# Weight sums in two half buffers, one-input softmax statistics, loads on ACT's queue and C21 of a pair in PSUM, in a one-core diffusion step

## The chip, the cores and the metric

The kernel runs on one core of a Trainium2 chip. The metric is the device time of one execution in microseconds (us). The engines are called PE (TensorE), PEld (its weight loads), DVE (VectorE), ACT (ScalarE), POOL (GpSimd) and SP (SyncE, which here only issues transfers).

## The reference, cut to what matters

One layer with two head groups that read the same normalised input: a gated position-mixing MLP (group A) and latent attention with four heads (group B). Their outputs are concatenated, go through the output projection `w_o`, are gated and added to the residual, and the rows are normalised.

```python
def _back(x, gate, a_out, attn, g_b, w_o):
    y = jnp.concatenate([a_out, attn * jax.nn.silu(g_b)], axis=-1) @ w_o
    return x + gate * y
...
    attn = _block_attention(qn, (qr_rot, qr), ((kn, kr_rot, vv), (kn_c, kr_c, v_c)))
    xs = _back(xs, gate, a_out, attn, g_b, w_o[l])
y_prompt = _rmsnorm(xp, final_g)
y_sample = _rmsnorm(xs, final_g)
```

There are 1024 latent rows (8 tiles of 128), 128 context rows (tile 8) and 256 cached keys. All is float32.

## The kernel before, in words

Products are made in three passes over a high and a low part of each operand (`hi` is a rounded copy, `lo = x - hi`), so nearly every product has a copy (ACT or POOL) and a subtraction (DVE) ahead of it.

**Softmax and value stage** (lines 1450 to 1780, some 317 to 540 us of the span). For each of 32 heads (8 tiles x 4), PE makes logits against 1024 latent and 256 context keys. `softmax` takes two maxima on DVE (L1480, L1483), joins them to the bias `nb` (L1484), ACT makes two exponentials with their sums (L1490), DVE adds the sums and inverts them (L1494, L1495), and POOL scales the row `e` (L1496). `value_steps` transposes `e` on PE (L1557), splits the result into `ph` (ACT, L1561) and `pl` (DVE, `lo_of`, L112), multiplies by the values (L1581 to L1583) and projects (L1600). The order on each engine is the order in which the program issues instructions. It is written by hand: every step has a cost, `later(dt, fn)` puts a step off by that much planned time, and `merged` mixes two lists of steps in proportion to their costs. An engine then runs its instructions in that order, each as soon as what it needs is there.

**Weight sums**. The output projection of the latent tiles is done on pairs of tiles by a scheme with seven products instead of eight (A11, A12, S4, S2, S1, S3, A22) on sums of blocks of `w_o`. The four sums T1 to T4 are made during the softmax stage, in 16 pieces, the *units* `(u, part)`: u counts eight slices of `w_o`, a part is two subtractions on POOL (`t_unit`, `sub`, L809). The raw slices lie in the tile `traw` (two buffers). After part 1 the kernel copies the high parts into `thi` (ACT, L1883), subtracts in place (DVE, L112) and stores both parts to `tdram` with eight transfers on SP (L1880). `divide`, once per head, starts the units: one and two in turn, as long as there are any. The tile pool of the sums is closed after head 17, and then the pieces of plain `w_o` are loaded and split, as *jobs* in the list `his` (copies on POOL) and `los` (subtractions on DVE), a few per head. Jobs of `w_o` have rank 0 and go ahead of others.

**Start of the last stage**. The context tile 8 is projected in the plain way, `plain(k, i)` for k of eight weight blocks and i of two column halves, into two PSUM banks `wps[8]`; the first two products of pair 0 are made beside it (the list `early`, mixed with the last two value streams). `t_piece` and `t_fetch` load the weight sums back from `tdram`, issued by POOL (L1901, L1905): T2 early, T3 after `plain(4, 1)`, T1 and T4 at the start of the last stage. Gates, the rows `xr` and `final_g` are loaded by SP (L1987, L2047, L2059).

**Last stage** (from line 2015, 536 us to the end). A small planner, `Plan`, holds steps with an engine, a planned cost, what they depend on, a priority and resources they take and give. At each planned instant it issues the first step in order of priority whose engine is free, whose inputs are made and whose resources are left. It only fixes the order of issue. Resource `w` counts PSUM banks (pool `psw`, five banks), `raw` PSUM copies of blocks, engine `D` the loads, which follow each other every 1.35 planned us (`fetch`). For each pair `pair(n)` makes seven products on PE; the queue of split blocks runs up to five ahead (`hi`, `raw`, `lo` of queue entry q). DVE adds the products up to C11, C12, C22 and C21 (`c11`, `c12`, `c22`, `c21`), each is gated (`m..`) and added to its row (`a..`), mostly on POOL, and ACT squares the row for the norm (`square`, L2078). `norm` makes the root, and `y` scales the two rows (DVE, L2110) and stores them. The last pair has another order and an end written out by hand (`finish`, L2260 to L2305).

```python
on_v(D_("c21"), lambda: add(V, K, ps("A22"), K), [P_("A22"), D_("k7")], 2, gives=("w",))
on_g(D_("m21"), lambda: G.tensor_tensor(K, K, gL(), op=ALU.mult), [D_("c21"), "gate0"], 3)
on_g(D_("a21"), lambda: add(G, half(b, L), half(b, L), K), [D_("m21"), f"x{b}"], 3)
square(b, 1, lambda: K, L, [D_("a21")])
```

Of the kernel before, what the change touches and what calls it, by code (L numbers as in the profile page):

```python
# [18 lines left out]
P = 128  # L19
# [75 lines left out]
def tile_hymba_step(ctx: ExitStack, tc: tile.TileContext, I, O):  # L95
# [1374 lines left out]
    def softmax(t, h, lat_, con_):  # L1470

        m = sm.tile([P, 2], F32, tag="m", name=f"m{t}{h}", bufs=3)
        nb = sm.tile([P, 1], F32, tag="nb", name=f"nb{t}{h}", bufs=3)
        su = sm.tile([P, 2], F32, tag="su", name=f"su{t}{h}", bufs=3)
        rs = sm.tile([P, 1], F32, tag="rs", name=f"rs{t}{h}", bufs=3)
        e = ap_.tile([P, 1280], F32, tag="e", name=f"e{t}{h}", bufs=6)
        es[t, h] = e

        def start():
            V.tensor_reduce(m[:, 0:1], lat_, axis=AX.X, op=ALU.max)  # L1480

        def shift():
            V.tensor_reduce(m[:, 1:2], con_, axis=AX.X, op=ALU.max)  # L1483
            V.scalar_tensor_tensor(nb, m[:, 0:1], m[:, 1:2], nscl[:, t : t + 1], op0=ALU.max, op1=ALU.mult)  # L1484
            later(0.6, exps)
            later(1.3, lambda: spare_lo(1))

        def exps():
            for i, (src, sl) in enumerate(((con_, slice(1024, 1280)), (lat_, slice(0, 1024)))):
                S.activation(e[:, sl], src, AF.Exp, bias=nb, scale=scl[:, t : t + 1], accum_out=su[:, i : i + 1])  # L1490
            later(2.5 if t == 0 or (t, h) < (1, 2) else 1.9, divide)

        def divide():
            V.tensor_tensor(rs, su[:, 0:1], su[:, 1:2], op=ALU.add)  # L1494
            V.reciprocal(rs, rs)  # L1495
            G.tensor_scalar(e, e, rs, 0.0, op0=ALU.mult, op1=ALU.add)  # L1496
            made.add(("e", t, h))
            spare_hi(2)
            spare_lo(2)
            if units and units[0][0] in traw:  # L1500
                n_ = min(len(units), (1, 2)[paced[0] % 2])
                paced[0] += 1
                for _ in range(n_):
                    unit_of[0](*units.pop(0))

        return start, shift
# [276 lines left out]
    with tc.manual_schedule(engines=engines):  # L1783
# [73 lines left out]
        th, tl = {}, {}  # L1857
# [7 lines left out]
        def t_unit(u, part):  # L1865

            k, c = divmod(u, 2)
            raw = traw[u]
            b11, b12, b21, b22 = (raw[:, i, :] for i in range(4))
            if part == 0:  # L1870
                sub(G, b11, b12, b11)
                sub(G, b12, b22, b12)
                return
            sub(G, b22, b22, b11)
            sub(G, b21, b21, b22)
            hi = tp.tile([P, 4, 256], F32R, tag="hi", name=f"thi{u}")

            def store(i, src):
                for m, j in ((1, 0), (3, 1), (4, 2), (2, 3)):
                    nc.sync.dma_start(f32(tdram[m - 1, k][:, i, 256 * c : 256 * c + 256]), src[:, j, :])  # L1880

            def high(i):
                S.copy(hi[:, 2 * i : 2 * i + 2, :], raw[:, 2 * i : 2 * i + 2, :])  # L1883
                if i:
                    store(0, f32(hi))

            def low(i):
                lo_of(raw[:, 2 * i : 2 * i + 2, :].bitcast(F32R), raw[:, 2 * i : 2 * i + 2, :], hi[:, 2 * i : 2 * i + 2, :])
                if i:
                    store(1, raw)  # L1890
                    if u + 2 < 8:
                        t_load(u + 2)
# [52 lines left out]
        for c in range(len(pairs)):  # L1945
# [18 lines left out]
            if 2 * c + LEAD + 1 == 17:  # L1964
# [20 lines left out]
        def load_xr(t):  # L1985
            xr[t] = ep.tile([P, 1024], F32, tag="xr", name=f"xr{t}", bufs=4)
            nc.sync.dma_start(xr[t], I["x"][t])  # L1987
# [37 lines left out]
    plan.resources.update(w=1, raw=2)  # L2025
# [9 lines left out]
    def on_g(key, fn, deps, prio, cost=1.3, **kw):  # L2035
        step(key, "G", cost, fn, deps, prio, lag=0.15, **kw)
# [8 lines left out]
    def load_gate(cond, **kw):  # L2045
        gate[cond] = ep.tile([P, 1024], F32, name=f"gate{cond}", **kw)
        nc.sync.dma_start(  # L2047
# [11 lines left out]
    fetch("fg", lambda: nc.sync.dma_start(fg, I["final_g"].broadcast_to([P, 1024])))  # L2059
# [29 lines left out]
    def norm(g, prio, by_half=False):  # L2089
# [17 lines left out]
        for i, u in enumerate(g):  # L2107
# [5 lines left out]
            if not by_half:  # L2113
                on_v(f"y{u}", scale, [*prev, "fg"], prio, 1.25)
# [49 lines left out]
    def pair(n):  # L2164
# [46 lines left out]
        if last:  # L2211
# [3 lines left out]
            step(f"free{n}", "N", 0.0, lambda: None, [f"sq{a}.0"], 0, gives=("w",))  # L2215
# [6 lines left out]
        if not last:  # L2222
# [9 lines left out]
            on_v(D_("c21"), lambda: add(V, K, ps("A22"), K), [P_("A22"), D_("k7")], 2, gives=("w",))  # L2232
            on_g(D_("m21"), lambda: G.tensor_tensor(K, K, gL(), op=ALU.mult), [D_("c21"), "gate0"], 3)
            on_g(D_("a21"), lambda: add(G, half(b, L), half(b, L), K), [D_("m21"), f"x{b}"], 3)
            square(b, 1, lambda: K, L, [D_("a21")])
# [176 lines left out]
```

## Time and profile before

| | us |
|---|---|
| three runs | 626.41, 629.21, 631.53 (median 629.21) |
| the profiled execution: time, span | 629.55, 627.8 |
| PE busy | 600.1 of the span |
| DVE, ACT, POOL busy | 427.5, 329.9, 218.1 |
| granted TensorE clock, mean | 0.992 |

In the rows of a timeline stand the start (us from the span's start), the duration, the engine, the line, the operation, output and inputs, shapes, and in brackets the idle time of the engine before it with what ended it. Rows of one line that follow each other are merged and counted (x2). In the rows of windows stand the window, its length, the busy time of PE, PEld, DVE, ACT and POOL with the number of instructions, the granted clock, the share of the 16 transfer engines and GB/s. Matmuls are pipelined: a PE that is busy all the time issues a 512-column matmul every 0.23 us, though each lasts 0.39.

### The profile page before, as it was taken

The page shows a single profiled execution, that of the slowest core. Times are in us where ns is not written, and L with a number is a line of the kernel's source. Part 1 is how long each engine was busy: PE and PEld are TensorE (multiplying, and loading weights), DVE is VectorE, ACT ScalarE, POOL GpSimd, SP SyncE. Part 2 cuts the span into 40 slices and gives each one's busy share as a digit, 9 for nine tenths or more (in the row PEclk, how much of TensorE's full clock was granted, in tenths as well). Part 3 has the DMA queues.
Part 4 walks back from the last instruction along what each step waited for, and adds up shares of the span by engine and source line. Part 5 has one row for each costly group of instructions (what it writes and reads, how often), then busy time and mean ns, then how long its engine had stood idle before and what let it go on. Part 6 is the DMA issues. An engine that isn't in the chain of part 4 may idle for free. (4 is left out here: it accounts for less than half of the span.)

```text
span 627.8 us, 10196 instructions
## 1 busy us (share of the span) xinstructions
PE 600.1 (96%) x3659; PEld 538.9 (86%) x3659; DVE 427.5 (68%) x911; ACT 329.9 (53%) x765; POOL 218.1 (35%) x261
## 2 busy tenths in 40 slices
PE   8899999999999999999999989899999999989992
PEld 7578889999989999999988978789999988768882
DVE  4784458896855567566778677786766855458765
ACT  6556754336423354555675656566555443456543
POOL 2451111000000000433462455552332566558772
PEclk9999999999999999999999999999999999989997
DMA  8992000101261034000020063651101028944222
GB/s 318 389 367 72 1 33 2 34 1 67 101 232 62 11 119 131 13 1 1 6 69 1 27 215 130 202 167 35 68 2 34 33 85 267 367 154 168 88 101 114
DMA packets 31922, 67.33 MB, mean 107 GB/s; under 512 B 3440, under 2 KB 18560, under 8 KB 31360
## 3 DMA queue, kind: packets, MB, share of 16 engines
q1 hardware_dynamic: 28560, 57.50, 26.5%
q0 software_dynamic: 2880, 8.39, 4.1%
q10 hardware_dynamic: 432, 0.79, 0.3%
q8 instruction: 29, 0.48, 0.3%
q14 instruction: 21, 0.17, 0.1%
HBM read 53.45 MB, written 13.21 MB: 106 GB/s over the span
## 5 line engine op out<-in xcount | busy, mean ns | idle before, releaser
L1496 POOL TENSOR_SCALAR e<-e,rs 128x1280 f32<-128x1280 f32 x32 | 46.2, 1444 | 105.5 <-DVE rs L1495 49.3
L112 DVE TENSOR_TENSOR pl<-pT,ph 128x512 fp32r<-128x512 f32 x81 | 55.4, 687 | 39.3 <-ACT ph L1561 37.9
L1490 ACT ACTIVATE e<-s,nb,scl 128x256 f32<-128x256 f32 x64 | 56.1, 880 | 39.8 <-DVE nb L1484 39.8
L1561 ACT CAST ph<-pT 128x512 fp32r<-128x512 f32 x80 | 46.0, 587 | 35.4 <-PE pT L1557 31.7
L1237 POOL TENSOR_TENSOR kr<-z,rope 128x64 f32<-128x64 f32 x8 | 2.6, 322 | 172.5 <-ACT z L1246 172.5
L1557 PE MATMUL pT<-ident,e 128*128 128x128 f32 x320 | 48.4, 274 | 6.8 <-DVE pl L112 6.8
L752 PE MATMUL tp<-area,w 128*128 128x384 f32 x288 | 52.4, 338 | 0.0
L752 PEld LDWEIGHTS tp<-area,w 128*128 128x128 f32 x288 | 50.3, 188 | 0.4
L1581 PE MATMUL o<-ph,vh 128*128 128x256 f32 x160 | 47.7, 298 | 0.0
L1557 PEld LDWEIGHTS pT<-ident,e 128*128 128x128 f32 x320 | 37.1, 140 | 12.1 <-PE at L1600 4.0
L1583 PE MATMUL o<-ph,vl 128*128 128x256 f32 x160 | 45.2, 282 | 0.0
L1582 PE MATMUL o<-pl,vh 128*128 128x256 f32 x160 | 45.1, 282 | 0.0
L1480 DVE TENSOR_REDUCE m<-s 128x1 f32<-128x1024 f32 x32 | 38.9, 1216 | 1.5 <-PE s L1514 1.5
L1510 PE MATMUL s<-kch,area 128*128 128x512 f32 (+2 forms) x100 | 39.0, 390 | 0.0
L1513 PE MATMUL s<-krh,area 128*128 128x512 f32 (+2 forms) x100 | 35.4, 354 | 0.0
L1511 PE MATMUL s<-kcl,area 128*128 128x512 f32 (+2 forms) x100 | 35.3, 353 | 0.0
L1512 PE MATMUL s<-kch,area 128*128 128x512 f32 (+2 forms) x100 | 35.2, 352 | 0.0
L1514 PE MATMUL s<-krl,area 128*128 128x512 f32 (+2 forms) x100 | 35.2, 352 | 0.0
L976 PE MATMUL tp<-area,w 128*128 128x384 f32 x192 | 35.0, 337 | 0.0
L976 PEld LDWEIGHTS tp<-area,w 128*128 128x128 f32 x192 | 33.6, 188 | 0.4 <-issue 0.4
L1581 PEld LDWEIGHTS o<-ph,vh 128*128 128x128 f32 x160 | 30.4, 190 | 1.6
L1582 PEld LDWEIGHTS o<-pl,vh 128*128 128x128 f32 x160 | 30.4, 190 | 1.4
(660 smaller groups left out, 1731.3 us busy)
## 6 DMA issues: line engine op xcount, KB each, us to landing
ada<-in_ada_ss SPq DMA_DIRECT2D x16, 512.0 KB, 8.5
w2r<-in_w_t SPq DMA_DIRECT2D x12, 512.0 KB, 4.5
x<-in_x SPq DMA_DIRECT2D x9, 512.0 KB, 7.9
xr<-in_x SPq DMA_DIRECT2D x9, 512.0 KB, 8.5
adag<-in_ada_g SPq DMA_DIRECT2D x4, 1024.0 KB, 5.0
traw<-in_w_o SPq DMA_DIRECT2D x16, 256.0 KB, 3.4
tdram<-thi SPq DMA_DIRECT2D x32, 128.0 KB, 3.0
tdram<-traw SPq DMA_DIRECT2D x32, 128.0 KB, 2.1
```

The lines of the kernel that those rows point to most:

```text
L112: V.tensor_tensor(lo, src, f32(hi), op=ALU.subtract)
L752: T.matmul(tps[i, g][:, :GW], w_[i][:, k, :], x_[k, g], start=k == 0 and j == 0, stop=k == NK - 1 and j == 2)
L976: T.matmul(tps[c, 2][:, :GW], w_[c][:, k, :], x_[k, 2], start=k == 0 and m == 0, stop=k == NK - 1 and m == 2)
L1480: V.tensor_reduce(m[:, 0:1], lat_, axis=AX.X, op=ALU.max)
L1490: S.activation(e[:, sl], src, AF.Exp, bias=nb, scale=scl[:, t : t + 1], accum_out=su[:, i : i + 1])
L1496: G.tensor_scalar(e, e, rs, 0.0, op0=ALU.mult, op1=ALU.add)
L1510: T.matmul(ps, qh_, kch[:, sl], start=True, stop=False)
L1557: T.transpose(ps[:, w : w + P], es[t, h][:, c * P : (c + 1) * P], ident)
L1561: later(0.5, lambda: S.copy(ph[:, :w], ps[:, :w]))
L1581: T.matmul(o, vh[:, kt, :], ph[:, sl], start=c == 0, stop=False)
L1582: T.matmul(o, vh[:, kt, :], pl[:, sl], start=False, stop=False)
L1583: T.matmul(o, vl[:, kt, :], ph[:, sl], start=False, stop=c == n - 1)
```

## The change

1. While there are units, the join of two maxima and the sum of two exponential sums, which read two tensors, become reductions over the two columns; the factor of `nb` is an instruction of its own.
2. The high copies of a unit get a tile for each half (`hi0`, `hi1`), and stores go out by half. The first half is copied 3.6 planned us after part 0, the rest after part 1. Units are started 1, 1, 1, 2 per head instead of 1, 2; the second of two is put off by 2.2. The pool is closed after head 19.
3. `plain(0..3, 1)` come first in `early`, and T3 is fetched by four jobs of `his`, entered after `plain(3, 1)` behind the jobs of rank 0.
4. Gates, rows 8, 0 and 1 and `final_g` are issued by ACT instead of SP.
5. C21 of pairs 0 to 2 is added up in the PSUM bank of A22, gated and added to its row by DVE, and the bank is given back after the square.
6. A resource `lock` of one keeps planned POOL steps and the scaling of output rows `y` apart.

```diff
         def shift():
             V.tensor_reduce(m[:, 1:2], con_, axis=AX.X, op=ALU.max)
-            V.scalar_tensor_tensor(nb, m[:, 0:1], m[:, 1:2], nscl[:, t : t + 1], op0=ALU.max, op1=ALU.mult)
+            if units:
+                V.tensor_reduce(nb, m, axis=AX.X, op=ALU.max)
+                V.tensor_scalar(nb, nb, nscl[:, t : t + 1], None, op0=ALU.mult)
+            else:
+                V.scalar_tensor_tensor(nb, m[:, 0:1], m[:, 1:2], nscl[:, t : t + 1], op0=ALU.max, op1=ALU.mult)
...
         def divide():
-            V.tensor_tensor(rs, su[:, 0:1], su[:, 1:2], op=ALU.add)
+            if units:
+                V.tensor_reduce(rs, su, axis=AX.X, op=ALU.add)
+            else:
+                V.tensor_tensor(rs, su[:, 0:1], su[:, 1:2], op=ALU.add)
...
-                n_ = min(len(units), (1, 2)[paced[0] % 2])
+                n_ = min(len(units), (1, 1, 1, 2)[paced[0] % 4])
                 paced[0] += 1
-                for _ in range(n_):
-                    unit_of[0](*units.pop(0))
+                for i in range(n_):
+                    unit_of[0](*units.pop(0), 2.2 * i)
...
-        def t_unit(u, part):
+        def t_unit(u, part, more):
...
+            def store(i, part_, src):
+                for m, j in ((1, 0), (3, 1), (4, 2), (2, 3))[2 * i : 2 * i + 2]:
+                    nc.sync.dma_start(f32(tdram[m - 1, k][:, part_, 256 * c : 256 * c + 256]), src[:, j % 2, :])
+
+            def high(i):
+                his_[u, i] = tp.tile([P, 2, 256], F32R, tag=f"hi{i}", name=f"thi{u}{i}")
+                S.copy(his_[u, i], raw[:, 2 * i : 2 * i + 2, :])
+                store(i, 0, f32(his_[u, i]))
+
+            def low(i):
+                half = raw[:, 2 * i : 2 * i + 2, :]
+                lo_of(half.bitcast(F32R), half, his_[u, i])
+                store(i, 1, half)
+                if i and u + 2 < 8:
+                    t_load(u + 2)
+
             if part == 0:
                 sub(G, b11, b12, b11)
                 sub(G, b12, b22, b12)
+                later(3.6 + more, lambda: high(0))
                 return
             sub(G, b22, b22, b11)
             sub(G, b21, b21, b22)
-            hi = tp.tile([P, 4, 256], F32R, tag="hi", name=f"thi{u}")
...
-            for i in range(2):
-                later(3.2 + 1.8 * i, lambda i=i: high(i))
-                later(4.6 + 1.8 * i, lambda i=i: low(i))
+            for dt, fn, i in ((2.6, low, 0), (3.6, high, 1), (5.2, low, 1)):
+                later(dt + more, lambda fn=fn, i=i: fn(i))
...
-            if 2 * c + LEAD + 1 == 17:
+            if 2 * c + LEAD + 1 == 19:
...
-            nc.sync.dma_start(xr[t], I["x"][t])
+            (nc.scalar if t in (8, 0, 1) else nc.sync).dma_start(xr[t], I["x"][t])
...
-            if k == 4 and i == 1:
-                for n in range(4):
-                    t_fetch(3, n, woh[n][:, 512:1024], wol[n][:, 512:1024])
-
-        early = []
+            if k == 3 and i == 1:
+                at_ = sum(1 for fn in his if rank.get(fn, 1) < 1)
+                his[at_:at_] = [lambda n=n: t_fetch(3, n, woh[n][:, 512:1024], wol[n][:, 512:1024]) for n in range(4)]
+
+        early = [(0.65, lambda k=k: plain(k, 1)) for k in range(4)]
         for k in range(7):
-            early += [(0.65, lambda i=i, k=k: plain(k, i)) for i in range(2)]
+            early.append((0.65, lambda k=k: plain(k, 0)))
+            if k >= 4:
+                early.append((0.65, lambda k=k: plain(k, 1)))
...
-    plan.resources.update(w=1, raw=2)
+    plan.resources.update(w=1, raw=2, lock=1)
...
-        step(key, "G", cost, fn, deps, prio, lag=0.15, **kw)
+        step(key, "G", cost, fn, deps, prio, lag=0.15, takes=("lock",), gives=("lock",), **kw)
...
-        nc.sync.dma_start(
+        nc.scalar.dma_start(
             gate[cond].rearrange(...)
...
-    fetch("fg", lambda: nc.sync.dma_start(fg, I["final_g"].broadcast_to([P, 1024])))
+    fetch("fg", lambda: nc.scalar.dma_start(fg, I["final_g"].broadcast_to([P, 1024])))
...
-                on_v(f"y{u}", scale, [*prev, "fg"], prio, 1.25)
+                on_v(f"y{u}", scale, [*prev, "fg"], prio, 1.25, takes=("lock",), gives=("lock",))
...
-            on_v(D_("c21"), lambda: add(V, K, ps("A22"), K), [P_("A22"), D_("k7")], 2, gives=("w",))
-            on_g(D_("m21"), lambda: G.tensor_tensor(K, K, gL(), op=ALU.mult), [D_("c21"), "gate0"], 3)
-            on_g(D_("a21"), lambda: add(G, half(b, L), half(b, L), K), [D_("m21"), f"x{b}"], 3)
-            square(b, 1, lambda: K, L, [D_("a21")])
+            on_v(D_("c21"), lambda: add(V, ps("A22"), ps("A22"), K), [P_("A22"), D_("k7")], 2)
+            on_v(D_("m21"), lambda: V.tensor_tensor(banks["A22"], banks["A22"], gate[0][:, L], op=ALU.mult), [D_("c21"), "gate0"], 2.5)
+            on_v(D_("a21"), lambda: V.tensor_tensor(xr[b][:, L], banks["A22"], xr[b][:, L], op=ALU.add), [D_("m21"), f"x{b}"], 2.5)
+            square(b, 1, lambda: banks["A22"], L, [D_("a21")])
+            step(f"free{n}", "N", 0.0, lambda: None, [f"sq{b}.1"], 0, gives=("w",))
```

More of the change, by code (lines that the diff above doesn't have):

```diff
@@ L1855, in need_lo @@
                     now[0] = now_
-        th, tl = {}, {}
+        th, tl, his_ = {}, {}, {}
         def t_load(u):
@@ L2214, in pair @@
             square(a, 0, lambda: banks["A12"], L, [D_("a11")])
-            step(f"free{n}", "N", 0.0, lambda: None, [f"sq{a}.0"], 0, gives=("w",))
+            step("free3", "N", 0.0, lambda: None, [f"sq{a}.0"], 0, gives=("w",))
         else:
```

13 lines of the change are left out of this document (removed).

## The prediction

> **What bounds the kernel now.** The first part of the page and the windows of 20 us say it: TensorE (PE) is busy 96% of the span, so time can only be won where PE is idle or its clock is low.
>
> ```profile
> span 627.8 us, 10196 instructions
> PE 600.1 (96%) x3659; PEld 538.9 (86%) x3659; DVE 427.5 (68%) x911; ACT 329.9 (53%) x765; POOL 218.1 (35%) x261
> 360.00:380.00 20.00, 17.39 (x118) 15.55 (x117) 15.36 (x30) 12.03 (x26) 10.66 (x11) 1.00 0.62 198
> 440.00:460.00 20.00, 20.00 (x140) 18.37 (x139) 15.11 (x31) 10.39 (x22) 6.22 (x6) 1.00 0.15 53
> 540.00:560.00 20.00, 17.33 (x68) 13.21 (x67) 12.52 (x20) 9.14 (x20) 13.35 (x13) 0.91 0.77 272
> 580.00:600.00 20.00, 20.00 (x90) 16.57 (x89) 13.02 (x23) 12.11 (x29) 15.70 (x13) 1.00 0.32 105
> ```
>
> The columns after each window's length are the busy us of PE, PEld, DVE, ACT and POOL (instructions in brackets), granted clock, DMA share and GB/s. Softmax work with the weight sums in it (360 to 380) leaves PE idle 2.6 us of 20; the same work without them (440 to 460) leaves none. In the last stage PE loses 2.7 us and clock around 554 us, then nothing until the tail. So I looked at three places: the waits of PE in the softmax stage, the start of the last stage, the tail.
>
> **The change part by part. Softmax stage.** The view of waits gives what PE waits for; the other rows are the timelines of PE, ACT, DVE and POOL.
>
> ```profile
> PE pT L1557 <- DVE pl L112: 6.5, 9, 1.1
> 341.80 0.63 PE L1557 MATMUL pT<-ident,e 128*128 128x128 f32 x4 [0.93 <-DVE pl L112]
> 364.12 0.63 PE L1557 MATMUL pT<-ident,e 128*128 128x128 f32 x4 [0.73 <-DVE pl L112]
> 374.12 0.66 PE L1557 MATMUL pT<-ident,e 128*128 128x128 f32 x4 [1.14 <-DVE pl L112]
> 370.50 0.62 ACT L1883 CAST thi<-traw 128x512 fp32r<-128x512 f32 x1 [2.82 <-DMA tdram<-traw]
> 361.81 1.55 POOL L809 TENSOR_TENSOR traw<-traw 128x256 f32<-128x256 f32 x2
> 362.73 0.65 DVE L1484 SCALAR_TENSOR_TENSOR nb<-m,nscl 128x1 f32<-128x1 f32 x1
> 441.61 0.22 DVE L1484 SCALAR_TENSOR_TENSOR nb<-m,nscl 128x1 f32<-128x1 f32 x1
> ```
>
> Nine waits cost 6.5 us. The one at 341.80 comes before the first weight sum and stays, which leaves 6.5 - 0.93 = 5.6 us. Two things feed them. First, the maximum `nb` takes 0.65 us while POOL subtracts (361.81 to 363.36) and 0.22 when POOL is quiet; the exponentials and the next split wait behind it. Second, the cast `thi` sat 2.82 us in ACT's order, ahead of exponentials, because one buffer holds both halves until all its stores have landed; the wait of 1.14 us follows.
>
> The change answers both: the cast has a buffer for each half, whose two stores went out a whole unit earlier; the maximum reads one tensor at a time; and units come at 1, 1, 1, 2 per head, 13 heads in place of 11, so most heads carry one cast and one subtraction. The price of the two-instruction `nb` comes from the nearest small one-input instructions beside POOL:
>
> ```profile
> 253.59 0.25 POOL L1238 TENSOR_TENSOR kr<-z,rope 128x32 f32<-128x32 f32 x1
> 253.65 0.15 DVE L1213 TENSOR_SCALAR zv<-ssz 128x1 f32<-128x1 f32 x1 [3.02 <-ACT j L1195]
> 255.24 0.39 DVE L1218 SCALAR_TENSOR_TENSOR zr<-zt,zr 128x2 f32<-128x2 f32 x1
> L1213 DVE TENSOR_SCALAR zv<-ssz x18: 143/154/154, 247.8 to 310.0; 128x1 f32<-128x1 f32 x18
> ```
>
> A TENSOR_SCALAR of 128x1 that starts inside a POOL instruction takes 0.15 us, never over 154 ns in 18; a two-input one beside POOL takes 0.39. Two such steps make about 0.15 + 0.19 = 0.35 us: 0.3 less than 0.65, and 0.13 more than 0.22 where POOL is quiet. `rs` by a reduction costs what its addition did. Of the 5.6 us I take 3.8 back, since three of the 13 heads still carry two parts. The bounds: all 5.6 gained; or, with nothing helped and 0.13 us on the path of all 13 heads, 1.7 lost.
>
> The Trainium skill, page SBUF — State Buffer, section Who interferes with whom, says that `tensor_scalar` within SBUF can use two ports and then contends with GpSimd, while `tensor_reduce` never does on trn2. By it the second new instruction would still wait; the rows above speak against that for 128x1, and by the rule the part would bring about 1.8 us instead of 3.8.
>
> **Order of the context products and the third sum.** `plain(0..3,1)` now come first. The bank of that half is the late one:
>
> ```profile
> 509.93 0.50 PE L1938 MATMUL w<-area 128*128 128x512 f32 x1 [0.26 <-ACT e L1490]
> 511.11 0.50 PE L1938 MATMUL w<-area 128*128 128x512 f32 x1 [0.21 <-ACT e L1490]
> 512.32 0.66 PE L1557 MATMUL pT<-ident,e 128*128 128x128 f32 x4 [0.24 <-DVE pl L112]
> 525.49 0.62 POOL L115 TENSOR_SCALAR area<-wor 128x512 fp32r<-128x512 f32 x1 [4.88 <-DMA wor<-in_w_o]
> 526.05 4.29 POOL L1901 DMA_DIRECT2D area<-tdram  x8
> ```
>
> Half 0 could start at 509.93, half 1 at 511.11, after the last exponentials. With half 1 first, PE idles from about 509.67 to 511.1, 1.4 us, in place of 0.26 + 0.21 + 0.24 = 0.7: **0.7 us lost** (bounds 0, and 2.4 if the clock drops). The third sum's eight transfers enter the job list behind the six splits of the last `w_o` pieces, and POOL stands at 525.49 waiting for the last piece anyway. So they start at about 526.7 in place of 526.05, and the splits no longer wait 4.29 us behind them: nothing, hidden by 20 us of products before S3 uses them.
>
> **Loads on ACT's queue.** This is the start of the last stage:
>
> ```profile
> 535.93 1.09 SPq L2047 DMA_DIRECT2D gate<-gdram  x2
> 537.11 2.25 SPq L1987 DMA_DIRECT2D xr<-in_x  x3
> 544.00:546.00 2.00, 1.22 (x6) 0.68 (x4) 0.93 (x3) 0.91 (x2) 1.59 (x2) 1.00 1.08 406
> 547.60 0.57 POOL L1905 DMA_DIRECT2D vlt<-tdram  x1
> DMA to landing us min/median/max: 8.3/8.3/8.3
> 553.71 0.40 PE L1911 MATMUL A<-vht,ringB 128*128 128x512 f32 x1
> 555.94 0.65 PE L1909 MATMUL A<-vlt,ringB 128*128 128x512 f32 x1 [1.84 <-DMA vlt<-tdram]
> 559.38 0.49 PE L1911 MATMUL A<-area,ringC 128*128 128x512 f32 x1
> wor<-in_w_o SPq DMA_DIRECT2D x8, 512.0 KB, 3.3
> ```
>
> The last piece of the fourth sum (`vlt`) is issued at 547.60 and takes 8.3 us; an equal 512 KB of `w_o` at a quieter time takes 3.3. The transfer engines are full (406 GB/s): gates, three rows and `final_g`, 3 MB, were issued together at 536 to 540. The kernel placed them one by one in its plan, gate 0 at 5.4 us and the rest from 12.15 us; SP has nothing else to wait for and sends them at once, while ACT reaches them in its order. ACT's plan puts gate 0 behind the cast at 540.71, gate 1 before the one at 548.92, the rows around 550 to 553. That takes 2.5 MB out of the way of the sums. With `vlt` down to 5 us or less it lands by 552.6, and PE needs it at 553.71 + 0.23 = 553.94. Then the wait falls away (555.94 - 553.94 = 2.0 us), and so does the slow clock after it: eight steps from 555.94 to 559.38 at 0.43 us in place of 0.23 and part of a ninth, 1.7 us. With 0.1 for `vht`: **3.8 us gained**, bounds 0 and 4.6 (0.83 us more for the wait before 546).
>
> ACT pays six issues of 0.33 to 0.66 us; it is busy 9.14 of 20 us there, so they hide. The first delays the copies behind it, on which POOL's second sum and the fourth sum's next pieces wait, by 0.66 us; the landing above allows for that.
>
> The Trainium skill, page DMA: Bandwidth & Descriptors, section Issuing engines are not separate DMA queues, says that issuing on another engine saves only the issue time, since all run on the same 16 engines. By it this part would bring nothing: that is rival 1. My gain hangs on the later time, not on the queue.
>
> **C21 in PSUM, the lock, the tail.**
>
> ```profile
> 599.70 1.28 POOL L2233 TENSOR_TENSOR mixA<-mixA,gate 128x512 f32<-128x512 f32 x1
> 583.83 0.69 DVE L2217 TENSOR_TENSOR mixB<-A,gate 128x512 f32<-128x512 f32 x1
> 577.77 0.69 DVE L806 TENSOR_TENSOR mixA<-A,mixA 128x512 f32<-128x512 f32 x1
> 608.43 4.28 DVE L2110 SCALAR_TENSOR_TENSOR xr<-xr,fss,fg 128x1024 f32<-128x1024 f32 x2
> 573.18 1.27 DVE L2110 SCALAR_TENSOR_TENSOR xr<-xr,fss,fg 128x1024 f32<-128x1024 f32 x1
> 612.63 0.69 DVE L2263 TENSOR_TENSOR P<-S,gate 128x512 f32<-128x512 f32 x1
> ```
>
> Per pair two POOL instructions of 1.28 us become two DVE ones of 0.69, and A22's bank stays taken until the square, some 3 us longer. PE is full there, DVE at 13 of 20, and the bank is next needed two products (5.4 us) after A22's end: nothing. In the tail two output rows take 4.28 us on DVE beside POOL, against 2 x 1.27 alone, and the last chain starts behind them at 612.63. The lock keeps them off POOL's instructions, and the shorter norm chain lets them come before the tail: 4.28 - 2.54 = **1.7 us gained**, bounds 4.3 gained and 2.5 lost (rows pushed behind POOL, into the last chain).
>
> **The sum**, against the profiled execution's own 629.55 us (1.75 around its span; 0.34 above the median of 629.21): -3.8 + 0.7 - 3.8 + 0 - 1.7 = -8.6, so **621.0 us**.
>
> **The rivals.**
>
> 1. The transfers stay late: POOL issues the fourth sum behind its own waits and 8 us is its own pace. For it: `vlt` leaves only at 547.60. Against: 406 GB/s beside it. 629.55 - 4.8 = 624.8.
> 2. Softmax keeps its waits, because casts and subtractions cost PE whatever their order: 0.5 gained there, 624.3. Against: the clean 440 to 460 also has splits in it.
> 3. The two-input wait moves into TENSOR_SCALAR, the change not doing what it says: 1.8 in place of 3.8, 623.0.
> 4. **Slower**: A22's bank, held to its square, starves PE in each of three pairs. DVE does c21 1.07 us after the product now; it must then gate, add, and ACT square. It decides once the square ends over 5.4 us after the product. At 2.1 us of wait and 1.7 of slow clock, three times: -8.6 + 11.4, 632.4; at a whole product, 2.7 + 1.7, 634.2, and over 635.5 with the loads late too.
>
> **How the numbers follow.** Forecast 0.50, own range 617.5 to 623.5; rivals 0.17, 0.13, 0.10, 0.10. The lower end 616.5 takes the better bounds of softmax, loads and a little of the tail; the upper end 629.5 leaves out rival 4 and little else. One per cent, 6.3 us, is about what a measurement can tell here (three runs before lie between 626.41 and 631.53): faster means under 622.9. Five sixths of the forecast's chance, half of rival 3's and a sixth of rivals 1 and 2 make 0.53, and 0.03 for several bounds at once: 0.56. Slower takes most of rival 4: 0.08. The rest, 0.36, is within.
>
> **What would show it.** Right: PE waits under 3 us between 340 and 440; `nb` near 0.15 + 0.15 us with no cast waiting for stores; PE idle 1.4 us near 510; no PE wait for `vlt` and full clock from 550 to 560; two output rows of 1.3 us before the last gates. Wrong: new waits at the transposes, `nb`'s TENSOR_SCALAR over 0.4 us, a wait for `vlt` as long as now, or PE waiting for a bank between 556 and 605.

## Result and the profile after

The changed kernel takes 632.03 us (median of 16 runs, 631.20 to 633.76), the kernel before 628.66 us on the same chip (16 runs, 625.66 to 633.53). The ratio is 1.0056, 95% interval 1.0038 to 1.0074: **slower by 0.6%**, where 621.0 us was forecast. The profiled execution took 631.2 us, with a span of 629.4 us.

The windows of the changed kernel, with the columns of the prediction's, show that one loss of PE is gone and another is not:

```profile
360.00:380.00 20.00, 18.35 (x128) 16.65 (x126) 14.43 (x32) 11.91 (x25) 10.53 (x12) 1.00 0.44 138
...
540.00:560.00 20.00, 19.17 (x85) 15.54 (x84) 13.61 (x23) 10.10 (x21) 10.70 (x11) 1.00 0.87 297
580.00:600.00 20.00, 20.00 (x90) 16.57 (x89) 16.49 (x28) 13.98 (x33) 10.84 (x9) 1.00 0.28 103
```

From 540 to 560 PE now works 19.17 us at full clock (17.33 at 0.91 before). From 360 to 380 it still idles 1.65 us (2.6 before), and 1.6 to 2.1 us in each window from there to 440, where two of three were nearly full before. To size the softmax stage I take the start of the sixth and of the last of the 32 large exponentials in ACT's timeline, two rows of the changed kernel and two of the one before:

```profile
341.25 1.20 ACT L1494 ACTIVATE e<-s,nb,scl 128x1024 f32<-128x1024 f32 x1
...
511.32 1.20 ACT L1494 ACTIVATE e<-s,nb,scl 128x1024 f32<-128x1024 f32 x1
```

```profile
341.73 1.20 ACT L1490 ACTIVATE e<-s,nb,scl 128x1024 f32<-128x1024 f32 x1
...
509.77 1.20 ACT L1490 ACTIVATE e<-s,nb,scl 128x1024 f32<-128x1024 f32 x1
```

The stage took 170.07 us after and 168.04 before: 2.0 lost. The waits of ACT from 340 to 440 in the kernel before say what the casts of the weight sums stood for; then come the same waits of the changed kernel, with those of DVE's subtractions for the weight sums and of PE (us in total, times, longest us):

```profile
ACT thi L1883 <- DMA tdram<-thi: 4.6, 3, 2.8
ACT thi L1883 <- DMA tdram<-traw: 2.8, 1, 2.8
```

```profile
ACT thi L1883 <- POOL traw L809: 9.2, 7, 2.1
DVE traw L112 <- ACT thi L1883: 4.5, 3, 1.5
DVE traw L112 <- POOL traw L809: 2.2, 4, 0.8
PE pT L1564 <- DVE pl L112: 5.0, 5, 1.1
PE pT L1564 <- DVE rs L1499: 2.9, 5, 0.7
```

The waits for stores are gone, as predicted. In their place the casts wait 9.2 us, seven times, for POOL's subtraction of the same part, and DVE's subtractions wait 6.7 us for the casts and for POOL (2.1 before, for stores). PE waits 7.9 us (6.5 before). One head in the timelines of POOL, DVE, ACT and PE:

```profile
374.14 2.04 POOL L809 TENSOR_TENSOR traw<-traw 128x256 f32<-128x256 f32 x2
374.90 0.69 DVE L112 TENSOR_TENSOR traw<-traw,thi 128x512 fp32r<-128x512 f32 x1 [0.40 <-POOL traw L809]
376.40 0.56 ACT L1494 ACTIVATE e<-s,nb,scl 128x256 f32<-128x256 f32 x1 [2.65 <-DVE nb L1486]
377.11 0.63 PE L1564 MATMUL pT<-ident,e 128*128 128x128 f32 x4 [1.12 <-DVE pl L112]
382.84 0.62 ACT L1883 CAST thi<-traw 128x512 fp32r<-128x512 f32 x1 [2.12 <-POOL traw L809]
```

DVE's subtraction for the weight sums stands ahead of the maximum, waits 0.40 us for POOL, and the exponentials and PE's transposes come late behind it. At 382.84 it is the cast that holds up the exponentials, but only by 0.5 us, since their maximum was ready just then. The same happens at 396.86; behind the other five waiting casts the exponentials started as soon as the maximum was made. So most of the 9.2 us did not hold them up.

The last stage and the tail, in the timelines of PE, DVE, POOL and SP of the changed kernel, then SP's load of tile 6 and PE's last row of the kernel before:

```profile
590.05 0.15 DVE L2109 SCALAR_TENSOR_TENSOR fss<-smalls,fss 128x2 f32<-128x2 f32 x1
590.22 1.29 POOL L2231 TENSOR_TENSOR mixA<-mixA,gate 128x512 f32<-128x512 f32 x1 [1.90 <-DVE fss L2109]
...
596.70 2.47 DVE L2117 SCALAR_TENSOR_TENSOR xr<-xr,fss,fg 128x1024 f32<-128x1024 f32 x2
600.68 0.33 SPq L1992 DMA_DIRECT2D xr<-in_x  x1
604.86 0.69 DVE L2220 TENSOR_TENSOR xr<-A,xr 128x512 f32<-128x512 f32 x1 [3.16 <-DMA xr<-in_x]
609.51 1.28 POOL L806 TENSOR_TENSOR xr<-xr,mixA 128x512 f32<-128x512 f32 x1 [1.94 <-DMA xr<-in_x]
613.03 0.28 PE L1916 MATMUL A<-vlt,ringC 128*128 128x256 f32 x1
614.65 1.28 DVE L2117 SCALAR_TENSOR_TENSOR xr<-xr,fss,fg 128x1024 f32<-128x1024 f32 x1
618.61 1.27 DVE L2117 SCALAR_TENSOR_TENSOR xr<-xr,fss,fg 128x1024 f32<-128x1024 f32 x1
```

```profile
593.72 0.33 SPq L1987 DMA_DIRECT2D xr<-in_x  x1
...
615.50 0.28 PE L1911 MATMUL A<-vlt,ringC 128*128 128x256 f32 x1
```

PE ends at 613.31, 2.5 us earlier than before (615.78). But the span ends 16.1 us behind that, not 12.0. The scale of rows y2 and y3 is made at 590.2; they are scaled only at 596.70, behind four POOL steps, the first of them at 590.22. Tiles 6 and 7 can be loaded only into buffers that those rows give back, so these loads go out 7 us later (600.68 against 593.72), and DVE and POOL then wait for them 3.16 and 1.94 us. Rows y4 and y5 fall among the last gates (614.65, 618.61).

### The profile page after: what moved, and what is told of

Read it like the earlier page. It is cut to its first block, busy times and chain, and to the rows that moved or that the text cites. A ratio compares the mean times of both kernels' runs of the same rounds, so it can differ in the third digit from the quotient of the medians.

```text
span 629.4 us, 10201 instructions
## 1 busy us (share of the span) xinstructions
PE 598.6 (95%) x3659; PEld 539.7 (86%) x3659; DVE 428.6 (68%) x929; ACT 329.5 (52%) x765; POOL 211.0 (34%) x255
## 4 chain that ended last, share of the span: by engine, by line
PE 77%; DVE 8%; ACT 5%; DMA 3%; issue 3%; POOL 3%; SPq 1%; ACTq 0%; POOLq 0%; DVEq 0%
PE p L954 9%; PE tp L752 8%; PE tp L976 5%; PE pT L1564 3%; PE zacc L1390 2%; PE zacc L1389 2%; PE zacc L1391 2%; ACT e L1494 2%; PE o L1588 2%; PE o L1590 2%; PE o L1589 2%; PE s L1520 2%; PE s L1518 2%; PE S L1914 2%; PE s L1519 2%
## 5 line engine op out<-in xcount | busy, mean ns | idle before, releaser
L1503 POOL TENSOR_SCALAR e<-e,rs 128x1280 f32<-128x1280 f32 x32 | 44.6, 1394 | 108.3 <-DVE rs L1502 53.6
```

## The experiments

Times are medians; the ratio, with its 95% interval, is against the kernel before run beside each kernel on the same chip (medians of 628.30 to 629.27 us from round to round). "Stage" is the time between the two exponentials above, "tail" the time from PE's last end to the span's end, both from the profile; "casts" is how long ACT's casts `thi` waited for POOL and for a transfer between 340 and 440.

| kernel | us | ratio | stage | tail | casts: POOL, DMA |
|---|---|---|---|---|---|
| before | 628.66 | 1 | 168.0 | 12.0 | 0.6, 7.4 |
| changed | 632.03 | 1.0056 (1.0038 to 1.0074) | 170.1 | 16.1 | 9.2, 0 |
| e1 changed, no lock | 626.88 | 0.9970 (0.9956 to 0.9985) | 170.1 | 11.0 | 9.2, 0 |
| e2 changed, old softmax | 631.09 | 1.0033 (1.0014 to 1.0052) | 169.3 | 15.7 | 4.4, 4.4 |
| e3 before + loads on ACT | 626.26 | 0.9960 (0.9943 to 0.9977) | 167.4 | 12.3 | 0.2, 8.1 |
| e4 before + lock | 637.67 | 1.0141 (1.0113 to 1.0169) | 167.0 | 16.8 | 0.2, 4.1 |
| e5 changed, y0 to y3 first | 629.37 | 0.9996 (0.9979 to 1.0013) | 170.3 | 13.1 | 9.3, 0 |
| e6 e3 + C21 in PSUM | 625.50 | 0.9949 (0.9932 to 0.9966) | 169.2 | 11.1 | 4.4, 4.6 |
| e7 before + one-input steps | 628.57 | 1.0001 (0.9980 to 1.0021) | 167.0 | 12.0 | 0.4, 6.5 |
| e8 before + new weight sums | 629.18 | 1.0013 (0.9994 to 1.0032) | 169.2 | 12.0 | 8.9, 0 |
| e9 e6 + one-input steps | 624.09 | 0.9916 (0.9888 to 0.9945) | 167.7 | 11.7 | 0.4, 8.3 |
| e10 e9 + pace 1, 1, 1, 2 | 621.41 | 0.9867 (0.9837 to 0.9896) | 164.5 | 10.9 | 1.8, 0.5 |
| e11 e9 + new weight sums, old pace | 626.95 | 0.9960 (0.9943 to 0.9976) | 170.2 | 11.6 | 8.5, 0 |
| e12 e9 + new order of products | 625.10 | 0.9925 (0.9897 to 0.9954) | 168.2 | 11.7 | 5.8, 3.6 |
| e13 changed, old moments of casts | 625.78 | 0.9955 (0.9939 to 0.9971) | 164.5 | 15.9 | 1.4, 0 |
| e14 e10 + two buffers | 621.27 | 0.9883 (0.9855 to 0.9911) | 164.5 | 10.9 | 1.4, 0 |
| e15 before + pace | 626.74 | 0.9964 (0.9941 to 0.9986) | 164.9 | 12.0 | 1.9, 0.7 |
| e16 e10, ACT's loads at once | 622.02 | 0.9894 (0.9866 to 0.9922) | 164.5 | 11.0 | 1.8, 0.5 |
| e17 e3, ACT's loads at once | 626.42 | 0.9973 (0.9958 to 0.9989) | 168.7 | 11.9 | 3.5, 4.5 |
| e18 e10, loads on SP | 623.80 | 0.9940 (0.9918 to 0.9962) | 164.6 | 11.0 | 1.8, 0.5 |

### The lock: e1, e4, e5

e1 takes the lock out of the changed kernel, e4 puts it alone into the kernel before, e5 keeps it and lets four rows pass:

```diff
-    plan.resources.update(w=1, raw=2, lock=1)
+    plan.resources.update(w=1, raw=2)
-        step(key, "G", cost, fn, deps, prio, lag=0.15, takes=("lock",), gives=("lock",), **kw)
+        step(key, "G", cost, fn, deps, prio, lag=0.15, **kw)
-                on_v(f"y{u}", scale, [*prev, "fg"], prio, 1.25, takes=("lock",), gives=("lock",))
+                on_v(f"y{u}", scale, [*prev, "fg"], prio, 1.25)
```

```diff
-                on_v(f"y{u}", scale, [*prev, "fg"], prio, 1.25, takes=("lock",), gives=("lock",))
+                on_v(f"y{u}", scale, [*prev, "fg"], 0.9 if u < 4 else prio, 1.25, takes=("lock",), gives=("lock",))
```

e1: 

> The changed kernel with the lock taken out again and all else kept. Theory (the lock): in the changed kernel the rows y2 and y3 had their scale at 590.05 us and were scaled at 596.70, behind four POOL instructions; the loads of x6 and x7 wait for them and were issued at 600.68 and 606.08, and DVE then stood 3.16 us for x6. The distance from PE's last instruction to the end of the span is 16.1 us instead of 12.0. Without the lock y2 and y3 run by 593, x6 and x7 are issued by 597 and 602, the distance falls back to about 12 us, and the time is 632.0 - 4.1 = 627.9 us. Rival (the other edits make the tail long: A22's gate and sum on DVE, or loads that come late on ACT's queue): y2 and y3 move but the distance stays 15 to 16 us, and the time stays 631 to 632.

e4: 

> The kernel before with only the lock added. Theory: y2 and y3 fall behind POOL's instructions, x6 and x7 are loaded late, and the end comes about 4 us later: 632.7 us. Rival (the lock is harmless by itself and only hurts with the shortened norm chain): 627 to 629, with y2 and y3 within 2 us of where they were and y4 and y5 at 2.6 us in place of 4.28.

e5: 

> The changed kernel with its lock, but the output rows y0 to y3 are put ahead of POOL's steps in the plan (priority 0.9 in place of 3.5); y4 and y5 stay as they are. Two prices of the lock are told apart: late loads of x6 and x7, and y4 and y5 pushed into the last chain (1.28 + 1.27 us on DVE at 614.65 and 618.61). Theory (both): DVE's wait of 3.16 us for x6 goes, y2 and y3 run by 592 us, y4 and y5 stay in the last chain, so about half of the 5.2 us that taking the lock out brought: 629 to 630 us. Rival a (only the late loads count): 627. Rival b (only the rows in the last chain count): 632.

DVE's and SP's timelines of e1 (rows y2 to y5, then the loads of tiles 6 and 7), DVE's and SP's of e5 for the same rows and loads, and the waits of PE in e4:

```profile
584.82 1.28 DVE L2117 SCALAR_TENSOR_TENSOR xr<-xr,fss,fg 128x1024 f32<-128x1024 f32 x1
587.22 2.30 DVE L2117 SCALAR_TENSOR_TENSOR xr<-xr,fss,fg 128x1024 f32<-128x1024 f32 x1
603.97 1.44 DVE L2117 SCALAR_TENSOR_TENSOR xr<-xr,fss,fg 128x1024 f32<-128x1024 f32 x1
605.93 1.71 DVE L2117 SCALAR_TENSOR_TENSOR xr<-xr,fss,fg 128x1024 f32<-128x1024 f32 x1
...
588.81 0.33 SPq L1992 DMA_DIRECT2D xr<-in_x  x1
593.70 0.33 SPq L1992 DMA_DIRECT2D xr<-in_x  x1
```

```profile
589.09 1.28 DVE L2117 SCALAR_TENSOR_TENSOR xr<-xr,fss,fg 128x1024 f32<-128x1024 f32 x1
590.89 1.28 DVE L2117 SCALAR_TENSOR_TENSOR xr<-xr,fss,fg 128x1024 f32<-128x1024 f32 x1
610.85 1.28 DVE L2117 SCALAR_TENSOR_TENSOR xr<-xr,fss,fg 128x1024 f32<-128x1024 f32 x1
615.89 1.28 DVE L2117 SCALAR_TENSOR_TENSOR xr<-xr,fss,fg 128x1024 f32<-128x1024 f32 x1
...
593.09 0.33 SPq L1992 DMA_DIRECT2D xr<-in_x  x1
598.48 0.33 SPq L1992 DMA_DIRECT2D xr<-in_x  x1
```

```profile
PE A L1909 <- DVE smalls L2096: 3.0, 1, 3.0
```

Without the lock the time falls by 5.2 us with PE ending where it did (613.43): the whole loss of the tail is the lock's. Part of the delay of y2 and y3 comes ahead of the hold: in e1 their scale is made at 584.7, in the changed kernel at 590.2, so the lock also puts off steps that the norm needs. e5 gives back 2.7 us by the earlier rows and loads (3.8 by the ratios), and no engine waits for the rows of tiles 6 and 7 any more. What is left to e1 is 2.5 us (1.6 by the ratios). In e5 y4 and y5 still stand among the last gates, which fits the theory of two prices, but these two rows were not moved by themselves. Alone in the kernel before, the lock costs 9.0 us, more than I expected (4). There the load of tile 6 goes out at 608.75, DVE stands 5.5 us for it, and PE's wait of 3.0 us ends right behind. POOL has two steps more per pair, which may keep the rows waiting longer, but that was not tried by itself. The rows y2 to y5 do take about 1.28 us each under the lock, as meant; two of the earlier rows still take 2.34 and 1.94 in the changed kernel. But without the lock, behind C21 on DVE, y4 and y5 take 1.44 and 1.71, so there was hardly anything left for it to save.

### The softmax stage: e2, e7, e8, e9, e10, e11, e13, e14, e15

e2 puts the whole stage back in the changed kernel; e7 has only the one-input maximum and sum; e8 only the new weight sums with their pace; e9 is the sum of what had gained by then (e6 and e7); e10 and e11 split e8 into its pace and its inner order on top of e9; e15 has the pace alone; e13 and e14 have two buffers at the old moments. The edits of e10 and e15 (pace) and of e13 (moments):

```diff
-                n_ = min(len(units), (1, 2)[paced[0] % 2])
+                n_ = min(len(units), (1, 1, 1, 2)[paced[0] % 4])
...
-            if 2 * c + LEAD + 1 == 17:
+            if 2 * c + LEAD + 1 == 19:
```

```diff
-                later(3.6 + more, lambda: high(0))
                 return
...
-            for dt, fn, i in ((2.6, low, 0), (3.6, high, 1), (5.2, low, 1)):
-                later(dt + more, lambda fn=fn, i=i: fn(i))
+            for dt, fn, i in ((3.2, high, 0), (4.6, low, 0), (5.0, high, 1), (6.4, low, 1)):
+                later(dt, lambda fn=fn, i=i: fn(i))
```

e2: 

> The changed kernel with the softmax stage and the weight sums as before (two-input maximum and sum, one buffer, units of 1 and 2 in turn). Theory: the new pace lost time there, PE at 341 was 0.48 us earlier than before and at 509 it was 1.55 us later, so the stage cost 2.0 us: the time falls to 630.0, and PE's events near 509 lie 2.0 us earlier than in the changed kernel. Rival (the stage's loss does not reach the end, since the late rows in the tail set it): PE's events lie earlier, but the time stays 632.

e7: 

> The kernel before with only the one-input maximum and sum of the softmax, units and buffers as before. Theory (the maximum's wait for POOL was a part of the waits of PE, 0.3 us less on heads with a subtraction beside): the stage from the sixth exponentials to the last, 168.1 us before, falls by 0.5 to 2, the time to 627 to 628. Rival (the waits of PE hang on the casts and the order, not on the maximum): 168 us and 628.7.

e8: 

> The kernel before with only the new weight sums: a buffer for each half, casts and stores moved, units at 1, 1, 1, 2 per head; two-input maximum and sum as before. Theory (the new pace is what lost the time in the softmax stage: casts ahead of POOL's subtraction of the same unit, on more heads): the stage from the sixth exponentials to the last grows from 168.1 to 170.5 us or more, the time to 631. Rival (the one-input steps cost it, 0.13 us on each head): 168.1 us and 628.7.

e9: 

> The parts that gained so far, together: the kernel before with the loads on ACT's queue, C21 in PSUM and the one-input maximum and sum; no lock, weight sums and order of the products as before. Loads and C21 took 625.5 us with a stage of 169.2 us from the sixth exponentials to the last; the one-input steps alone had 167.0 where kernels with the old steps had 167.0 to 169.3 (mean 168.2 of five). Theory (the one-input steps shorten the stage where subtractions still stand beside the maximum): stage 167 us, 624.3 us. Rival (the stage's length varies by itself from run to run and the steps bring nothing): 625.5 us.

e10: 

> The kernel of the parts that gained, with the old weight sums spread at 1, 1, 1, 2 parts per head over 13 heads in place of 1 and 2 over 11. Theory a (a delay comes with every head that carries a part, so more heads cost more): the stage grows from 167 to 168.5 us or more and the time by 1.5. Theory b (the loss of the new weight sums lies in their inner order, the casts between exponentials and copies): stage and time within 0.5 us of the kernel of the parts that gained.

e11: 

> The kernel of the parts that gained, with the new weight sums (a buffer for each half, casts and stores of the first half moved to the head of part 0) at the old pace of 1 and 2 parts per head. Theory b (the inner order costs): stage 168.5 us or more, time 1.5 us above the kernel of the parts that gained. Theory a (the pace costs): within 0.5 us of it, or below, since no cast waits for a store.

e13: 

> The changed kernel whole, lock included, with two buffers and the pace 1, 1, 1, 2 kept, but the casts and DVE's subtractions at the moments of before: both halves 3.2 to 6.4 us behind the second part. Theory (the moments: ACT stood 9.2 us in 7 casts for POOL's subtraction, with exponentials and copies queued behind): those waits go, the stage from the sixth exponentials to the last falls from 170.1 to 165 us, the time from 632.0 to 627. Rival (the two buffers and the earlier stores cost it): stage 169 to 170 us, time 631 to 632.

e14: 

> The best kernel so far (loads on ACT's queue, C21 in PSUM, one-input steps, old weight sums at 1, 1, 1, 2; 621.4 us, stage 164.6 us) with a buffer for each half added, at the moments of before. Theory (the moments cost, the buffers don't): 164.6 us and 621.4, or 0.5 less, since one wait of 0.53 us for a store was left. Rival (buffers and earlier stores cost): stage 167 or more, 624.

e15: 

> The kernel before with only the pace 1, 1, 1, 2 and nothing else. In the best kernel the pace took the stage from 167.8 to 164.6 us, most of it the stores' waits of ACT's casts (8.3 us in four, then 0.5 in one). Theory (the pace does this alone): stage 165 to 166 us, 628.9 - 2.7 = 626.2. Rival (it needs the one-input steps, since more heads then have a subtraction beside the maximum): 168 us, 628.9.

Two of these theories fell. I had blamed the pace (e8, e10); e10 shows that **the pace gains**: the stage falls from 167.7 to 164.5 us, and alone (e15) from 168.0 to 164.9. The loss is in the inner order. e11, with the new order at the old pace, has 170.2 us. e13 decides it: with buffers, pace, lock and all else kept, only the moments of the casts and of DVE's subtractions put back, the stage goes from 170.1 to 164.5 us and the time from 632.03 to 625.78. The waits of ACT's casts and of PE from 340 to 440 in e13:

```profile
ACT thi L1883 <- POOL traw L809: 1.4, 1, 1.4
PE pT L1564 <- DVE pl L112: 1.8, 3, 0.9
PE pT L1564 <- DVE rs L1499: 0.7, 2, 0.4
PE pT L1564 <- DVE rs L1501: 0.2, 1, 0.2
```

PE's waits fall from 7.9 to 2.7 us, the casts' from 9.2 to 1.4, and DVE's subtractions for the weight sums no longer wait. e13 moves casts and subtractions together, so how the loss divides between them is not shown; the rows above speak for DVE's side, since only two casts held up exponentials, by 0.5 us each. Two buffers by themselves change nothing (e14 against e10): with the slower pace the stores have landed anyway, 0.5 us of waiting in one cast being left in e10. The one-input steps did what was said of the instruction, as the groups of DVE in e10 and in the kernel before show (340 to 440, mean ns of one behind the busy us):

```profile
L1486 DVE TENSOR_SCALAR nb<-nb,nscl 128x1 f32<-128x1 f32 x12 | 2.6, 214 | 0.4
L1485 DVE TENSOR_REDUCE nb<-m 128x1 f32<-128x2 f32 x12 | 1.9, 155 | 0.4
```

```profile
L1484 DVE SCALAR_TENSOR_TENSOR nb<-m,nscl 128x1 f32<-128x1 f32 x15 | 7.8, 520 | 0.5
```

0.37 us in place of 0.52 on the mean, but little of it reaches the time: e7 can't be told from the kernel before, e9 is 1.4 us faster than e6 with intervals that overlap, and at the new pace the stage is 164.9 us without these steps (e15) and 164.5 with them (e10). e2 shows only 0.9 us, since its own stage, with the old units, came out at 169.3: all kernels with the old units at the old pace lie between 167.0 and 169.3.

### The loads on ACT's queue: e3, e16, e17, e18

e3 is the kernel before with the diff's three `nc.scalar` lines. e16 and e17 issue the same loads on ACT, but all at once at the head of the stage; e18 puts them back on SP in e10:

```diff
+    def at_once(key, fn):
+        fn()
+        fetch(key, lambda: None)
...
-    fetch("gate1", lambda: load_gate(1, tag="xr", bufs=4))
+    at_once("gate1", lambda: load_gate(1, tag="xr", bufs=4))
```

e3: 

> The kernel before with only the loads of gates, three rows and final_g moved to ACT's queue. Theory: the wait for vlt and the slow clock after it go, as in the changed kernel, and all behind it moves up: 628.7 - 3.8 = 624.9 us, with 1.00 granted clock from 550 to 560 and 12 us from PE's last instruction to the end. Rival (the tail takes it back, because the rows for the last pair then come late against PE): 627 to 629 with 14 to 16 us behind PE's last instruction.

e16: 

> The best kernel so far with gates, rows and final_g still on ACT's queue, but issued at the head of the stage in one go, as SP did in the kernel before. Theory (the later issue is the gain, the queue is not): the transfers stand before vlt again, PE waits about 1.8 us for it, the granted clock drops behind it, and the time is 621.4 + 2.5 to 3.8 = 624 to 625. Rival (the queue is the gain): 621.4, no wait for vlt.

e17: 

> The kernel before with the loads on ACT's queue, but all issued at the head of the last stage, as SP did. Theory (the later issue is the gain): PE waits 1.5 to 2 us for vlt, the clock drops behind it, 628 to 629 us. Rival (the queue is the gain, since on SP's queue the loads stand behind the last pieces of w_o and end later): no wait for vlt, 626 to 627 us as with the planned issue (626.3).

e18: 

> The best kernel so far with gates, rows and final_g on SP's queue again. Theory (the loads' move is worth as much here as in the kernel before, 2.4 us): 621.4 + 2.4 = 623.8 us with PE waiting for vlt. Rival (the new pace moved the transfers and made the wait for vlt go by itself): 621.5 to 622, as with the loads at once on ACT's queue (622.0).

The move is worth 2.5 us in the kernel before (e3: 628.73 us beside it) and 2.4 in the best one (e18 against e10; 4.6 by the ratios), where PE waits 1.6 us for `vlt` again. But the later issue brings at most a part of it. In e16 the loads go out at once on ACT, PE does not wait for `vlt`, and the time is 622.02 (621.41 with planned issue; the intervals overlap). In e17 the loads go out at 536.03 to 539.50, as on SP before; here are ACT's and POOL's issues, the window before `vlt` lands, its time to landing, and PE's row:

```profile
536.03 1.07 ACTq L2051 DMA_DIRECT2D gate<-gdram  x2
549.30 0.57 POOL L1905 DMA_DIRECT2D vlt<-tdram  x1
550.00:552.00 2.00, 2.00 (x11) 1.65 (x10) 1.88 (x3) 0.84 (x2) 0.59 (x1) 1.00 1.17 418
DMA to landing us min/median/max: 5.5/5.5/5.5
554.87 0.50 PE L1909 MATMUL A<-vlt,ringB 128*128 128x512 f32 x1 [0.24 <-DMA vlt<-tdram]
```

The transfer engines are as full as before (418 GB/s), `vlt` even leaves 1.7 us later, behind ACT's 3.25 us of issues, which hold up its copies; yet it lands 1.1 us earlier (554.8 against 555.9) and PE waits 0.24 us, with no slow clock behind it. The time, 626.42, can't be told from that with planned issue. The Trainium skill, page DMA: Bandwidth & Descriptors, section Issuing engines are not separate DMA queues, has it that issuing on another engine saves only the issue time. e17, with equal moments of issue, ran at 0.9973 (0.9958 to 0.9989) of the kernel before, 1.9 us less by the medians. Whether that is the loads' own queue, against the page, or the order that ACT's delay makes on POOL, these runs don't settle.

The slow clock does not follow every such wait. In the traces PE's wait for `vlt` of 1.84 us (before) and of 1.91 (e15) is followed by a granted clock of 0.54 and 0.50 in the window from 556 to 558, while 2.09 us in e4 and 1.59 in e18 leave it at 1.00.

### C21 and the order of the products: e6, e12

e6 adds to e3 the change's five lines of C21, e12 adds to e9 its `plain` and `early`.

e6: 

> The kernel before with two parts of the change: loads on ACT's queue, and C21 in PSUM with its gate and sum on DVE; no lock, softmax and order as before. The kernel with the loads alone took 626.26 us with 12.3 us behind PE's last instruction; the changed kernel without the lock had 11.0 us there. Theory (C21 on DVE frees POOL, so y4 and y5 run earlier and less beside POOL): 626.3 - 1.2 = 625.1 us and 11 us behind PE. Rival (my predicted nothing for this part): 626.3 with 12 us behind PE. Rival (A22's bank held to its square starves PE): PE waits between 556 and 605, over 628.

e12: 

> The kernel of the parts that gained, with the order of the context products and the fetch of the third sum as in the change. My prediction put this at 0.7 us lost: PE's busy time from 500 to 520 was 19.29 of 20 us before and 18.98 in the changed kernel, which makes 0.3. Expected: 0.3 to 0.7 us above the kernel of the parts that gained, with one idle time of 1.0 to 1.4 us on PE ahead of the first product in place of three short ones. Rival (the order costs nothing to the end, as the tail takes it up): within 0.2 us, which these rounds can't tell from 0.3 by the times alone, so the rows of PE decide.

C21 in PSUM brought 0.8 us (626.26 to 625.50), which lies within the intervals; the tail, 11.1 us in place of 12.3, agrees. The rows y4 and y5, which take 4.57 us together in e3, take 1.38 and 1.55 in e6, and PE had no wait for a bank from 556 to 605 in e6 nor in the changed kernel. For the order, PE's waits from 505 to 516 in e9 and in e12:

```profile
508.83 0.50 PE L1945 MATMUL w<-area 128*128 128x512 f32 x1 [0.26 <-ACT e L1494]
510.02 0.50 PE L1945 MATMUL w<-area 128*128 128x512 f32 x1 [0.23 <-ACT e L1494]
511.22 0.65 PE L1564 MATMUL pT<-ident,e 128*128 128x128 f32 x4 [0.24 <-DVE pl L112]
```

```profile
508.72 0.50 PE L1945 MATMUL w<-area 128*128 128x512 f32 x1 [0.26 <-ACT e L1494]
511.11 0.66 PE L1564 MATMUL pT<-ident,e 128*128 128x128 f32 x4 [0.73 <-DVE pl L112]
```

0.73 us of idle time becomes 0.99: 0.3 lost, the foot of what was expected. The medians differ by 1.0 us with intervals that overlap.

## Why the prediction was wrong, step by step

| term | forecast | measured | by |
|---|---|---|---|
| softmax stage | -3.8 | +0.9 in time, +2.0 in the trace | changed against e2; stage 170.07 against 168.04 |
| order and third sum | +0.7 | +0.3 to +1.0 | e12 against e9 |
| loads on ACT's queue | -3.8 | -2.4 to -2.5, by the medians | e3, e18 |
| C21 in PSUM | 0 | -0.8 | e6 against e3 |
| lock and tail | -1.7 | +5.2 | changed against e1 |
| sum | -8.6 | +3.1 to +3.9 in time | 632.03 - 628.66 = +3.4 |

Two steps failed, each by more than 4 us; in a third, the loads, the sign was right and the reason given is not borne out.

**The lock** was costed by what it saves (4.28 - 2.54) and bounded by rows "pushed behind POOL, into the last chain, 2.5 lost". The bound named one price, y4 and y5 pushed into the last chain; what e5 leaves against e1, 1.6 to 2.5 us, is the most that these runs give it. It missed the other: what waits for a held step. The rows y2 and y3 give back the buffers for tiles 6 and 7, and with a priority of 3.5 against POOL's 1 to 3 they get the lock only when POOL has nothing to do. e5, which lets y0 to y3 pass, puts that price at 2.7 to 3.8 us. The saving was mis-sized too: C21's move, put at nothing, already brings it (4.57 us for the two rows in e3, 1.38 and 1.55 in e6).

**The softmax stage**: the remark that casts "have a buffer for each half, whose two stores went out a whole unit earlier" was true of the stores, and their wait did go. It did not ask what the cast at 3.6 planned us behind its subtraction meets: POOL makes it behind the large scaling of `e`, so the casts wait 9.2 us in ACT's order, and DVE's subtractions behind them wait 6.7 us in DVE's order, ahead of maxima and of the sums that PE's transposes need. The bound for a loss, "nothing helped", allowed no new wait. The gain was there all the same, and came from the part that I used only as a count of heads: the pace alone takes 3.1 us off the stage (e15), and the new moments of the casts and of DVE's subtractions then cost 5.6 (the changed kernel against e13). The one-input maximum, with most of my working behind it, is worth 0.4 us of stage at the new pace.

**The loads**: the wait for `vlt` went, but "My gain hangs on the later time, not on the queue" is not borne out: issued at once on ACT the loads bring most of it (e16, e17). One reason that the term was too large can be seen: 1.7 of its 3.8 us were a slow clock behind the wait, which the traces of e4 and e18 do not have although PE waits there.

**Sums.** Five sixths of 0.50, half of 0.10 and a sixth of 0.30 make 0.52, not 0.53. How 5.6 us of waits become 3.8 is not worked out there: ten of 13 heads would make 4.3.

**Rivals.** Rival 1 did not come about: the wait for `vlt` goes, and it lands 5.7 us after its issue, not 8. Rival 2 (the waits stay, whatever the order) is the nearest for that stage, but its reason is wrong, since the order is just what matters (e13). Rival 3 did not happen: TENSOR_SCALAR took 0.21 us with POOL busy or not (0.15 was forecast). The Trainium skill, page SBUF — State Buffer, section Who interferes with whom, says that `tensor_scalar` can enter a two-port mode, when its operands meet certain conditions, and can then contend with GpSimd; at 128x1 the rows show none of that. Rival 4 forecast 632.4, near the time measured, by a mechanism that isn't there: PE was 20.00 of 20 us busy from 580 to 600.

**Right**: the vanished wait for `vlt` and its slow clock, at two thirds of the price; PE's end 2.5 us earlier even with the stage's loss; the order's sign; C21 without a stall of PE; no stall at S3 for the third sum.

e10 and e14 beat both kernels: 621.41 us, 0.9867 (0.9837 to 0.9896) of the kernel before. They have the loads on ACT's queue, C21 in PSUM, the one-input steps and the new pace, and neither the lock nor the new moments.

## What to carry to other kernels

Cost a lock or a priority by what waits for the step it holds, buffers to be given back above all, not only by the step's own duration: here 1.7 us were to be saved and 5.2 were lost. When a step is moved earlier in an in-order engine, look up when its input is done on the other engine; a copy or subtraction issued too early puts its producer's delay in front of whatever stands behind it. Count a wait only where something behind it was ready: of the 9.2 us of the casts little held up an exponential. An edit that bundles pace, buffers and moments should be split before it is judged: one of the three gained 3 us of the stage, one did nothing, and one lost more than 5.

## What the runs showed of the hardware that I had not expected

The same loads, issued at the same moments by ACT instead of SP, left the transfer engines as full (418 GB/s from 550 to 552, 406 before). The last piece of the fourth sum left 1.7 us later and still landed 1.1 us earlier (e17). The length of PE's wait for it did not settle the clock behind it: 1.84 us in the kernel before was followed by matmuls of 0.43 us each in place of 0.23, and 2.09 us in e4 by a granted clock of 1.00.
